# Spreading the gMLP layer-norm statistics and bias over four steps, with reordered top-k, modulation-row and query-pack work, in a one-core decoder block

## The chip, the cores and the metric

The kernel runs on one core of a Trainium2 chip. The metric is the time of one execution in microseconds (us), the median of three runs. A run of before was also recorded by the hardware profiler, and all views below are of that one execution.

## The reference, cut to what matters

One decoder layer over 512 positions of width 1024. The input is normalised and modulated by rows that come from a conditioning vector, then projected into ten pieces. The part that the change touches is mixer A, the gated MLP, and what runs beside it:

```python
h = rms_norm(x, norm1_g) * (1.0 + scale1) + shift1
z = h @ w_in                       # a_u, a_v, q, k, v, qi, ki, wi, g_a, g_b
...
v = layer_norm(gelu(a_v), ln_g, ln_b).reshape(bsz, n, 128, 8, 128)
mixed = einsum('gts,bnsgc->bntgc', w_s * tril, v) + b_s
y_a = gelu(a_u) * mixed
...
sel_score, sel_idx = lax.top_k(score, 256)      # per query, indexer scores
y_b = attention of q over the selected keys
...
merged = sigmoid(g_a) * (y_a @ w_proj_a) + sigmoid(g_b) * (y_b @ w_proj_b)
x = x + gate1 * (merged @ w_out)
```

A feed-forward part and a final norm follow. The layer norm's shift `ln_b` reaches the mixed output as `ln_b` times the row sums of the masked `w_s`, so the kernel computes these row sums (`wrow`) and adds them to `b_s` instead of adding `ln_b` to v.

## The kernel before

All large products are fp32 products made of three matmuls in a rounded fp32 form. Each weight chunk of 128x1024 numbers (512 KB) is loaded by SyncE into one of three `raw` buffers (`issue`, L149), rounded by ScalarE to `hi` (L167), and VectorE or GpSimd subtracts `lo = raw - hi` (L171). `hi` and `lo` have three buffers each. `mm3` (L107 to L109) then issues, for each pair of blocks, hi by h-hi, hi by h-lo, and lo by h-hi: the third matmul is the first that needs `lo`. `opt_b` runs over the chunks of a weight group; before each chunk it calls the step's side tasks and then `get`, which prepares the chunks up to two ahead. So the preparation of the chunk after next is emitted behind a step's side tasks, and stands behind them in the queues of ScalarE and VectorE.

The stages around the change, in the order of the program:

- the a_v stage, 14 steps whose side tasks are in the table `VT`. Among them: `wn_load`, `wn_mask` and `wn_sum` form the row sums of the masked spatial weights; `wn_out` (L1043) writes them to a DRAM scratch, turned; `wn_in` reads them back, one copy per partition, into `wr`; `load_ws` and `load_bs` load spatial weights and bias; `ln_v(tk, 0)` takes the statistics of the first half of v's columns.
- the a_u stage, steps 0 to 7 of `au_tasks`, two chunks of each of four groups `W_AU`, 24 matmuls a step. Step 0 finishes the layer norm's statistics (`ln_v(tk, 1)` for four blocks of rows), takes the power -1/2 on GpSimd (`rstd`), forms `nmr` and scales the bias rows on ScalarE (`bias_a`, eight instructions). Steps 1 and 2 normalise v in place on ScalarE (`ln_v2`), and step 2 adds the bias (`bias_b`). After step 3 TensorE mixes the first group (`mix_mm`, L1183), the others after steps 4 to 9; `mix_ev` takes them out on VectorE (L1189, L1192 and a split).
- steps 8 to 23: gate A (`W_GA`) and the projection of y_a (`W_PA`), two chunks each in turn, four times. Attention begins in step 22 (`at_step`), with `qk` products on TensorE and the softmax's first row operation on VectorE (L1319).

Three things run in the background of these steps. The top-k search is a list `bg` of 32 items, alternately `topk_max` (three MAX8, L862) and `topk_replace` (three MATCH_REPLACE8, L866), and three closing items; `run_bg(us)` pops items until their nominal costs exceed its budget. The modulation rows of gate 1 and of the second norm are dot products: SyncE loads 512 KB into `mraw` (L255) and VectorE multiplies and sums (L259). `room` decides how early such a load is issued: two may be outstanding before, in two buffers that alternate. The rows of q that are rotated are packed through DRAM (`Packed`): `gather`, `fetch`, `turn` on VectorE, `put` and `scatter`, where all DMAs are issued by GpSimd.

SyncE works through its DMA list in order, and a DMA whose buffer isn't free yet holds the ones behind it.

Of the kernel before, what the change touches and what calls it, by code (L numbers as in the profile page):

```python
# [58 lines left out]
def block_kernel(ctx: ExitStack, tc: tile.TileContext, x, x_t, w_in,  # L59
# [3 lines left out]
    T, V, A, P, SY = nc.tensor, nc.vector, nc.scalar, nc.gpsimd, nc.sync  # L63
# [63 lines left out]
    def issue(i):  # L127
        e = stream[i]
        if e["kind"] == "m" and e["early"]:
            k = mrot[0]  # L130
            mrot[0] += 1
            raw = s2pair(k % 8, F32).rearrange("p a n -> p (a n)")
        elif i in last_raw:
            raw = last_raw[i]()
        elif e["kind"] == "m" and e["mid"]:
            k = e["mid"]
            if k == "A2":
                k = ("A2", "G1")[mrot[1] % 2]
                mrot[1] += 1
            raw = mid.tile([128, 1024], F32, name="mraw", tag=k, bufs=1)  # L140
        else:
            raw = base.tile([128, 1024], F32, name="raw", tag="raw", bufs=RAWB)
        e["raw"] = raw
        if e["kind"] == "m":
            e["dma"](raw)
            return
        k0, nk, n = e["kts"][0], len(e["kts"]), e["n"]
        e["view"] = lambda t: t[:, :nk * n].rearrange("p (j n) -> p j n", j=nk)
        SY.dma_start(raw[:, :nk * n], e["src"](k0, nk, e["c0"] if isinstance(e["c0"], tuple) else ((e["c0"], n),)))  # L149
        if i in W1[2:7]:  # L150
            load_xt(W1.index(i) + 1)
# [22 lines left out]
    def ensure(upto):  # L174
        upto = min(upto, len(stream) - 1, st["limit"] - 1)
        while True:
            for i in range(st["prep"], min(st["prep"] + 16, len(stream), st["limit"])):
                if "raw" in stream[i]:
                    continue
                if room(i):  # L180
                    issue(i)
                elif stream[i]["kind"] == "w" or not stream[i]["mid"]:
                    break
            if st["prep"] > upto:
                break
            prep(st["prep"])
            st["prep"] += 1

    def room(i):
        e = stream[i]  # L190
        if i in last_raw:
            return True
        pend = [stream[k] for k in range(st["prep"], i) if k not in last_raw]
        if e["kind"] == "m" and e["early"]:
            return sum(p["kind"] == "m" for p in pend) < 8
        if e["kind"] == "m" and e["mid"]:
            n = sum(p["kind"] == "m" for p in pend)
            return n < (2 if e["mid"] == "A2" else 1) and len(pend) <= 1 + 2 * n
        return sum(p["kind"] == "w" or not (p["early"] or p["mid"]) for p in pend) < RAWB


# [216 lines left out]
    V.tensor_copy(cols[:, 0:67], pack[:, 0:67])  # L418
    posi = pack[:, 67:195].bitcast(I32)
    P.tensor_copy(half_sum[:, 16:32], pack[:, 195:211])  # L420
    lng, lnb, wrow = half_sum[:, 16:24], half_sum[:, 24:32], half_sum[:, 32:40]

    ones = mid.tile([128, 128], F32, name="ones", tag="A3", bufs=1)
    P.memset(ones, 1.0)
# [241 lines left out]
    class Packed:  # L666

        def __init__(self, tag, srcs):
            self.srcs, self.rows = srcs, 32 * len(srcs)
            self.d = [dram.tile([128, S], F32, name=f"pk{tag}{k}") for k in range(2)]  # L670

        def part(self, k, n):
# [10 lines left out]
        def fetch(self):  # L683
            t = at_line(base, "S2_4", (2, S), F32, "pk") if self.rows < 64 else mid.tile(
                [128, 2, S], F32, name="pk", tag="G0", bufs=1)
            self.a, self.b = t[:, 0], t[:, 1]
            for o, flip in ((self.a, 0), (self.b, 1)):
                for h in range(2):
                    k = self.rows * (h ^ flip)
                    src = self.d[0][k:k + self.rows]  # L690
                    if self.rows < 64:
                        src = src[None].to_broadcast([2, 32, S])
                    P.dma_start(o[64 * h:64 * h + 64], src)

        def turn(self):
            V.tensor_mul(self.b, self.b, tab["q"][:, 1])
# [1 line left out]
            V.tensor_add(self.a, self.a, self.b)  # L698

        def put(self):  # L700
            P.dma_start(self.d[1], self.a)

        def scatter(self):
            for j, t in enumerate(self.srcs):
                for h in range(2):
                    P.dma_start(t[16 * h:16 * h + 16], self.rows_of(1, 128, j, h))

    kf = mid.tile([128, 2, S], F32, name="kf", tag="A0", bufs=1)
    mid.tile([128, 16], F32, name="pad")
# [56 lines left out]
    def k_b(h):  # L766
        if not kk:
            k_tiles()
        split(kk[0][:, h], kk[1][:, h], kf[:, h])
        A.activation(k_pl[:, h], kf[:, h, :128], AF.Copy)  # L770
# [238 lines left out]
    def av_sum(g, key):  # L1009
        avr[g, key] = t = avr[g, {"T2": "T1", "T4": "T2"}[key]]  # L1010
        V.tensor_add(t, t, avr[g, {"T2": "B22", "T4": "B21"}[key]])

    def av_w(g, key):
        hi, lo = (base.tile([128, 4, 256], F32R, name=n, tag=n, bufs=3) for n in ("hi", "lo"))
        split(hi, lo, avr[g, key])
        avw[g, key] = (hi, lo)
# [22 lines left out]
    def wn_sum(h):  # L1039
        for k in range(4):  # L1040
            A.activation(wn[:, k], wn[:, k], AF.Copy, accum_out=wrow[:, 4 * h + k:4 * h + k + 1])

    def wn_out():  # L1043
        P.dma_start(wsd.rearrange("m t -> t m"), wrow)

    def wn_in():
        late["wr"] = mid.tile([128, 1024], F32, name="wr", tag="G1", bufs=1).rearrange("p (a n) -> p a n", a=8)
# [30 lines left out]
    def ln_v(tk, h):  # L1078
        V.bn_stats(bst[:, tk, h * 6:h * 6 + 6], vg[tk // 2][:, tk % 2, h * 512:(h + 1) * 512])
        if h:  # L1080
            V.bn_aggr(mva[:, tk], bst[:, tk, 0:12])
# [24 lines left out]
    def av_add(k, op, src):  # L1106
# [8 lines left out]
          5: [lambda: av_w(1, "B11"), pkk.put, lambda: wn_load(1)],  # L1115
          6: [lambda: av_w(1, "T1"), lambda: av_acc(1, "T3"), lambda: issue(W_AU[0][0])],
          7: [lambda: av_sum(1, "T2"), lambda: av_w(1, "T2"), pkk.scatter, wn_mask],
          8: [lambda: av_w(1, "B21"), lambda: wn_sum(1), wn_out],
          9: [lambda: av_w(1, "T3"), lambda: av_sum(1, "T4")],
          10: [lambda: av_w(1, "B22"), wn_in],  # L1120
          11: [lambda: av_w(1, "T4"), lambda: issue(W_AU[0][1]), lambda: ln_v(0, 0)],
          12: [lambda: ensure(W_AU[0][0]), lambda: ln_v(1, 0), lambda: ln_v(2, 0), load_ws, load_bs],
          13: [lambda: ensure(W_AU[0][1]), lambda: ln_v(3, 0), lambda: k_b(0), ws_mask]}

    def av_post(g, p):
        if p == 0:
# [80 lines left out]
    def au_tasks():  # L1207
        s = austep[0]
        austep[0] += 1
        if s == 0:  # L1210
            k_b(1)
        for fn in PT.get(s, []):
            fn()
        if s == 0:
            for tk in range(4):
                ln_v(tk, 1)
            rstd(rva, mva[:, :, 1], 4, 1.0)
            V.scalar_tensor_tensor(nmr, mva[:, :, 0], -1.0, rva, op0=OP.mult, op1=OP.mult)
            bias_a()
            run_bg(0.8)  # L1220
        elif s == 1:
            ln_v2(0)
            ln_v2(1)
        elif s == 2:
            ln_v2(2)
            ln_v2(3)
            bias_b()
        for m in AT.get(s - 1, []):
            mix_ev(m)
        if s > 0:  # L1230
            run_bg(1.6 if s < 8 else 2.0)
        if s in (20, 21):
            at_split(s - 20)

# [1056 lines left out]
```

## Time and profile before

| what | value |
|---|---|
| median of three runs | 790.62 us (789.58 to 792.36) |
| the profiled execution's own time | 790.31 us |
| its span, first to last instruction | 788.6 us |
| outside the span | 1.7 us |
| mean granted TensorE clock | 0.995 |
| busy: TensorE, VectorE, ScalarE, GpSimd | 771.6, 669.3, 448.3, 195.0 us |

TensorE (PE) has an instruction in flight for 98% of the span. VectorE is DVE in the views, ScalarE ACT, GpSimd POOL, SyncE SP; "SPq" and "POOLq" are their DMA issues. In a timeline row stand the start, the duration, the engine, the line, the instruction and the tiles, and in brackets how long the engine sat idle before it and what it waited for. TensorE's matmuls overlap: one of 512 columns is shown as 0.39 us long, while the next starts 0.23 us after it. The time lost to a late operand is therefore read from start to start.

### The profile page before, as it was taken

What the parts mean: (1) busy time and instruction counts of PE and PEld (TensorE: products, weight loads), DVE (VectorE), ACT (ScalarE), POOL (GpSimd) and SP (SyncE); (2) the same over time, 40 slices, a digit from 0 to 9 for tenths busy, and PEclk for the clock granted to TensorE, in tenths of its full rate; (3) what the DMA queues carried; (4) which work ended last, traced back from release to release, by engine and by line L of the source; (5) the groups of instructions that cost most, each with busy time, mean ns of one, the idle gap of its engine ahead of it and who ended that gap; (6) DMA issues with size and microseconds to landing.
All of it is one profiled execution on the core that took longest, in us unless ns stands there. A gap on an engine that the chain in (4) does not pass through costs nothing.

```text
span 788.6 us, 12719 instructions
## 1 busy us (share of the span) xinstructions
PE 771.6 (98%) x4723; PEld 692.3 (88%) x4723; DVE 669.3 (85%) x1108; ACT 448.3 (57%) x803; POOL 195.0 (25%) x274
## 2 busy tenths in 40 slices
PE   8999999989999999999999999999999999999995
PEld 6899899968888788998888899999999999888884
DVE  8879777898999758986697878989999888998886
ACT  6665567553231346666546577655566666666653
POOL 5882312132365521200020000313121212000002
PEclk9999999999999999999999999999999999999998
DMA  9966655525264848627682503879896977666662
GB/s 349 416 188 188 151 155 144 169 88 171 101 195 162 289 163 213 188 63 272 213 254 35 206 1 108 247 234 299 257 279 208 270 211 188 180 193 210 206 214 107
DMA packets 54561, 153.45 MB, mean 195 GB/s; under 512 B 15617, under 2 KB 16257, under 8 KB 54498
## 3 DMA queue, kind: packets, MB, share of 16 engines
q1 hardware_dynamic: 41552, 115.34, 43.4%
q0 software_dynamic: 12368, 36.33, 19.1%
q10 hardware_dynamic: 578, 0.95, 0.3%
q8 instruction: 37, 0.61, 0.3%
q14 instruction: 26, 0.21, 0.1%
HBM read 146.29 MB, written 28.72 MB: 222 GB/s over the span
## 4 chain that ended last, share of the span: by engine, by line
PE 81%; DVE 12%; DMA 2%; ACT 2%; issue 1%; POOL 1%; POOLq 0%; SPq 0%; ACTq 0%; DVEq 0%
PE R L108 8%; PE R L107 8%; PE R L109 8%; PE pb L109 5%; PE pb L108 5%; PE pb L107 5%; PE pfo L108 4%; PE pfo L109 4%; PE pfo L107 4%; DVE sco L866 3%; DVE m L862 2%; PE pgb L107 2%; PE pgb L108 2%; PE pgb L109 2%; DVE mraw L259 2%; PE po L107 2%
## 5 line engine op out<-in xcount | busy, mean ns | idle before, releaser
L167 ACT ACTIVATE hi<-raw 128x1024 fp32r<-128x1024 f32 (+4 forms) x98 | 98.6, 1010 | 87.0 <-PE pfo L109 23.6
L171 DVE TENSOR_TENSOR lo<-raw,hi 128x1024 fp32r<-128x1024 f32 (+2 forms) x71 | 84.9, 1198 | 25.6 <-ACT hi L167 25.5
L109 PE MATMUL pb<-h,lo 128*128 128x512 f32 (+1 forms) x192 | 73.9, 385 | 3.5 <-DVE lo L171 3.4
L107 PE MATMUL pb<-h,hi 128*128 128x512 f32 (+1 forms) x192 | 74.3, 387 | 0.0
L108 PE MATMUL pb<-h,hi 128*128 128x512 f32 (+1 forms) x192 | 73.7, 384 | 0.0
L171 POOL TENSOR_TENSOR lo<-raw,hi 128x1024 fp32r<-128x1024 f32 x19 | 48.0, 2533 | 63.1 <-ACT hi L167 63.1
L108 PE MATMUL pfo<-lo,za 128*128 128x512 f32 (+1 forms) x144 | 55.2, 383 | 0.0
L109 PE MATMUL pfo<-hi,za 128*128 128x512 f32 (+1 forms) x144 | 55.2, 383 | 0.0
L107 PE MATMUL pfo<-hi,za 128*128 128x512 f32 (+1 forms) x144 | 55.2, 383 | 0.0
L259 DVE CUSTOM_DVE_ANT_0 mraw<-mraw,csb,cols 128x1024 f32<-128x1024 f32 x27 | 43.2, 1601 | 6.2 <-DMA mraw<-in_w_shsc_dram 6.2
L109 PEld LDWEIGHTS pb<-h,lo 128*128 128x128 f32 x192 | 36.5, 190 | 10.9 <-DVE lo L171 4.0
L107 PE MATMUL R<-tb,sx 128*128 128x256 f32 x160 | 44.2, 276 | 0.0
L109 PE MATMUL R<-tb,sx 128*128 128x256 f32 x160 | 44.2, 276 | 0.0
L108 PE MATMUL R<-tb,sx 128*128 128x256 f32 x160 | 44.2, 276 | 0.0
L107 PE MATMUL R<-tb,hi 128*128 128x256 f32 x160 | 44.2, 276 | 0.0
L108 PE MATMUL R<-tb,hi 128*128 128x256 f32 x160 | 44.2, 276 | 0.0
L109 PE MATMUL R<-tb,lo 128*128 128x256 f32 x160 | 44.2, 276 | 0.0
L392 POOL COPY sm<-sm 128x1 f32<-128x1 f32 x36 | 23.8, 660 | 81.6 <-ACT sm L391 81.6
L108 PEld LDWEIGHTS pb<-h,hi 128*128 128x128 f32 x192 | 36.5, 190 | 6.2
L107 PEld LDWEIGHTS pb<-h,hi 128*128 128x128 f32 x192 | 36.4, 189 | 6.0
L372 POOL DMA_DIRECT2D wsum<-in_w_ffn_out_dram x24 | 19.6, 816 | 74.5 <-DMA wsum<-wsum 42.2
L107 PEld LDWEIGHTS pfo<-hi,za 128*128 128x128 f32 x144 | 27.1, 188 | 5.4
(426 smaller groups left out, 2672.9 us busy)
## 6 DMA issues: line engine op xcount, KB each, us to landing
raw<-in_w_ffn_in_dram SPq DMA_DIRECT2D x44, 512.0 KB, 6.4
raw<-in_w_in_dram SPq DMA_DIRECT2D x38, 512.0 KB, 4.3
wsum<-in_w_ffn_out_dram POOLq DMA_DIRECT2D x30, 512.0 KB, 7.7
mraw<-in_w_shsc_dram SPq DMA_DIRECT2D x27, 512.0 KB, 6.5
raw<-wsum SPq DMA_DIRECT2D x20, 512.0 KB, 3.6
s<-in_w_shsc_dram SPq DMA_DIRECT2D x14, 512.0 KB, 8.3
raw<-in_w_ffn_out_dram SPq DMA_DIRECT2D x13, 512.0 KB, 3.7
wsum<-wsum POOLq DMA_DIRECT2D x10, 512.0 KB, 6.7
```

Of the source, the lines that this page charges most:

```text
L107: T.matmul(o, wh, rh, start=start, stop=False, **kw)
L108: T.matmul(o, wh, rlo, start=False, stop=False, **kw)
L109: T.matmul(o, wlo, rh, start=False, stop=stop, **kw)
L167: A.activation(hi[:, :m], e["raw"][:, :m], AF.Copy)
L171: e["lo"].tensor_sub(lo[:, :m], e["raw"][:, :m], f(hi[:, :m]))
L259: V.tensor_tensor_reduce(out=raw[:, c], in0=raw[:, c], in1=(csb if s > 1 else pc)[:, c], scale=scale, scalar=sums.pop(0), op0=OP.mult, op1 ...
L372: P.dma_start(wsum_at(n, c), src, max_dma_last_dim=4096, accum_op=OP.add)
L392: P.tensor_copy(t, t)
L862: V.max(m8s[i], sco[i])
L866: V.match_replace(out=sco[i], in_to_replace=m8s[i], in_values=sco[i], imm_value=TAKEN)
```

## The change

Five edits, all between the a_v stage and step 23:

1. The second-half statistics are spread: blocks 0 and 1 in step 0, blocks 2 and 3 and the power in step 1, `nmr`, the first normalisation and the scaled bias rows in step 2, the second normalisation and the bias add in step 3. Before, statistics, power, `nmr` and scaled bias were all in step 0, and each normalisation a step earlier.
2. The row sums are accumulated in `gcol`, turned in 32x32 blocks on VectorE, and written out as four DMAs of rows instead of one DMA of single numbers. `wn_out`, `wn_in` and `load_bs` move a step later, and the mask of the spatial weights moves to step 0 of a_u.
3. The top-k budget is 0 in step 0 and 1.3 in steps 1 to 6 (one item a step, where there were two), and 2.0 from step 7 on.
4. `room` allows a modulation-row load only when no other is pending, so each is asked for one period later.
5. The fetch, put and scatter DMAs of the two query packs are issued by SyncE; those of the key pack and all gathers stay on GpSimd.

The core of the diff:

```diff
@@ room
         if e["kind"] == "m" and e["mid"]:
-            n = sum(p["kind"] == "m" for p in pend)
-            return n < (2 if e["mid"] == "A2" else 1) and len(pend) <= 1 + 2 * n
+            return all(p["kind"] == "w" for p in pend) and len(pend) <= 1
...
-    lng, lnb, wrow = half_sum[:, 16:24], half_sum[:, 24:32], half_sum[:, 32:40]
+    lng, lnb, wrow = half_sum[:, 16:24], half_sum[:, 24:32], gcol[:, 16:24]
@@ Packed
+            self.q = P if tag == "k" else SY
...
-                    P.dma_start(o[64 * h:64 * h + 64], src)
+                    self.q.dma_start(o[64 * h:64 * h + 64], src)
...
-            P.dma_start(self.d[1], self.a)
+            self.q.dma_start(self.d[1], self.a)
...
-                    P.dma_start(t[16 * h:16 * h + 16], self.rows_of(1, 128, j, h))
+                    self.q.dma_start(t[16 * h:16 * h + 16], self.rows_of(1, 128, j, h))
@@
     def wn_out():
-        P.dma_start(wsd.rearrange("m t -> t m"), wrow)
+        V.transpose(gturn, gcol)
+        rows = wsd.rearrange("m (b j) -> m b j", j=32)
+        for b in range(4):
+            P.dma_start(rows[:, b], gturn[32 * b + 16:32 * b + 24])
@@ VT
-          8: [lambda: av_w(1, "B21"), lambda: wn_sum(1), wn_out],
-          9: [lambda: av_w(1, "T3"), lambda: av_sum(1, "T4")],
-          10: [lambda: av_w(1, "B22"), wn_in],
-          11: [lambda: av_w(1, "T4"), lambda: issue(W_AU[0][1]), lambda: ln_v(0, 0)],
-          12: [lambda: ensure(W_AU[0][0]), lambda: ln_v(1, 0), lambda: ln_v(2, 0), load_ws, load_bs],
-          13: [lambda: ensure(W_AU[0][1]), lambda: ln_v(3, 0), lambda: k_b(0), ws_mask]}
+          8: [lambda: av_w(1, "B21"), lambda: wn_sum(1)],
+          9: [lambda: av_w(1, "T3"), lambda: av_sum(1, "T4"), wn_out],
+          10: [lambda: av_w(1, "B22")],
+          11: [lambda: av_w(1, "T4"), lambda: issue(W_AU[0][1]), lambda: ln_v(0, 0), wn_in],
+          12: [lambda: ensure(W_AU[0][0]), lambda: ln_v(1, 0), lambda: ln_v(2, 0), load_ws],
+          13: [lambda: ensure(W_AU[0][1]), lambda: ln_v(3, 0), lambda: k_b(0), load_bs]}
@@ au_tasks
         if s == 0:
+            ws_mask()
             k_b(1)
...
-            for tk in range(4):
-                ln_v(tk, 1)
+            ln_v(0, 1)
+            ln_v(1, 1)
+        elif s == 1:
+            ln_v(2, 1)
+            ln_v(3, 1)
             rstd(rva, mva[:, :, 1], 4, 1.0)
+        elif s == 2:
             V.scalar_tensor_tensor(nmr, mva[:, :, 0], -1.0, rva, op0=OP.mult, op1=OP.mult)
-            bias_a()
-            run_bg(0.8)
-        elif s == 1:
             ln_v2(0)
             ln_v2(1)
-        elif s == 2:
+            bias_a()
+        elif s == 3:
             ln_v2(2)
             ln_v2(3)
             bias_b()
...
-            run_bg(1.6 if s < 8 else 2.0)
+            run_bg(1.3 if s < 7 else 2.0)
```

How the instructions stand on VectorE at the start of the a_u stage, before. `kin` holds the statistics, `mva` mean and variance, `m` and `sco` belong to the top-k search, and the `lo` here is that of the third chunk, which step 2 multiplies with:

```order
L1079 BN_STATS kin<-vg_1147 128x6
L1081 BN_AGGR mva<-kin 128x2
L1079 BN_STATS kin<-vg_1147 128x6
L1081 BN_AGGR mva<-kin 128x2
L1218 SCALAR_TENSOR_TENSOR sm<-mva,sm 128x4
L862 MAX m_1813<-sco_633 128x8
L862 MAX m_1815<-sco_632 128x8
L862 MAX m_1817<-sco_631 128x8
L171 TENSOR_TENSOR lo<-raw,hi 128x1024
L866 MATCH_REPLACE sco_633<-m_1813,sco_633 128x512
```

The same place now, from the first block's statistics on:

```order
L1082 BN_STATS kin<-vg_1146 128x6
L1084 BN_AGGR mva<-kin 128x2
L1082 BN_STATS kin<-vg_1146 128x6
L1084 BN_AGGR mva<-kin 128x2
L171 TENSOR_TENSOR lo<-raw,hi 128x1024
L1082 BN_STATS kin<-vg_1147 128x6
L1084 BN_AGGR mva<-kin 128x2
L1082 BN_STATS kin<-vg_1147 128x6
L1084 BN_AGGR mva<-kin 128x2
L862 MAX m_1838<-sco_633 128x8
L862 MAX m_1840<-sco_632 128x8
L862 MAX m_1842<-sco_631 128x8
```

The third chunk's `lo` has moved ahead of two of the four statistics, the `nmr` instruction (which waits for GpSimd's power) and the MAX8 triple. On ScalarE, at the same place, now: the normalisation (`vg`) of step 2 stands behind the first gelu output `u`, and the eight scaled bias rows `wr` behind the first normalisation:

```order
L167 ACTIVATE hi<-raw 128x1024 x2
L1245 ACTIVATE u<-pb 128x512 x2
L1174 ACTIVATE vg_1146<-vg_1146,sm 128x1024 x2
L1055 ACTIVATE wr<-wr,half_sum 128x128 x8
L167 ACTIVATE hi<-raw 128x1024
L1174 ACTIVATE vg_1147<-vg_1147,sm 128x1024 x2
L167 ACTIVATE hi<-raw 128x1024
L1245 ACTIVATE u<-pb 128x512 x2
```

Before, the eight `wr` came ahead of the third chunk's `hi`, and both normalisations ahead of the second `u`. On GpSimd the `lo` subtractions of steps 3 to 21 had the query packs' DMAs between them before:

```order
L171 TENSOR_TENSOR lo<-raw,hi 128x1024 x2
L706 DMA qf_602<-pkq_613 16x2x512 x2
L706 DMA qf_603<-pkq_613 16x2x512 x2
L693 DMA pk<-pkq_1150 64x512 x4
L171 TENSOR_TENSOR lo<-raw,hi 128x1024 x4
```

Now one row stands there, `lo` nineteen times over, and the DMAs are in SyncE's list between the weight loads. TensorE's order is the same in both kernels.

## Prediction

> **What bounds the kernel now.** I read the page's head, then TensorE's waits, then the chain of waits, then the timelines around the places those named.
>
> ```profile
> span 788.6 us, 12719 instructions
> PE pb L109 <- DVE lo L171: 3.4, 1, 3.4
> PE pb L109 <- POOL lo L171: 1.4, 1, 1.4
> ```
>
> After its start TensorE sits idle twice, both times for a `lo`, until the end of the span. So the change can gain only what the two cost, and whatever TensorE loses too briefly to be listed. Since matmuls overlap, I measure from start to start. TensorE's timeline around the first wait:
>
> ```profile
> 160.96 0.39 PE L107 MATMUL pb<-h,hi 128*128 128x512 f32 x1
> 161.19 0.39 PE L108 MATMUL pb<-h,hi 128*128 128x512 f32 x1
> 165.00 0.50 PE L109 MATMUL pb<-h,lo 128*128 128x512 f32 x1 [3.42 <-DVE lo L171]
> ...
> 166.08 0.63 PE L107 MATMUL pb<-h,hi 128*128 128x512 f32 x1
> 166.51 0.63 PE L108 MATMUL pb<-h,hi 128*128 128x512 f32 x1
> ...
> 169.44 0.39 PE L109 MATMUL pb<-h,lo 128*128 128x512 f32 x1
> ```
>
> A matmul normally starts 0.23 us after the last (160.96 to 161.19). Step 2 of a_u starts at 160.96, and its third matmul is late. From 161.19 to 169.44 there are 13 starts: 8.25 us where 13 x 0.227 = 2.95 would do. **5.3 lost**, of which 1.4 because seven matmuls behind the wait follow each other at 0.43, a halved clock. The other two places:
>
> ```profile
> 233.61 0.39 PE L108 MATMUL pb<-h,hi 128*128 128x512 f32 x1
> 234.08 0.50 PE L109 MATMUL pb<-h,lo 128*128 128x512 f32 x1
> ...
> 261.19 0.40 PE L108 MATMUL pb<-y,hi 128*128 128x512 f32 x1
> 262.98 0.50 PE L109 MATMUL pb<-y,lo 128*128 128x512 f32 x1 [1.40 <-POOL lo L171]
> ```
>
> The first loses 0.47 - 0.23 = **0.24**, the second 1.79 - 0.23 = **1.56**. All three make 7.1 us.
>
> The chain of waits tells why the two `lo` are late:
>
> ```profile
> 136.25 10.28 DMA wrow<-half_sum
> ...
> 162.34 1.47 DVE m L862 x3
> 163.82 1.12 DVE lo L171
> ...
> 204.00 1.59 DVE sco L866 x4
> ...
> 210.95 1.59 DVE sco L866 x4
> ...
> 249.81 2.67 DVE mraw L259
> 252.52 0.33 SPq L255
> 252.94 6.37 DMA raw<-in_w_proj_a_dram
> ```
>
> Step 0's statistics, GpSimd's power and a MAX8 triple stand ahead of the third chunk's `lo`; earlier, the write of the row sums as single numbers takes 10.28 and holds up GpSimd's list. The later wait comes through SyncE: a row load (L255) is issued only when VectorE, running late, has consumed that buffer (249.81 to 252.48), and the weights for step 18 are queued behind it.
>
> **The change, part by part.** A step has 24 matmuls, 24 x 0.227 = 5.45 us. VectorE's and ScalarE's timelines in step 0 and 1:
>
> ```profile
> 157.49 0.69 DVE L1079 BATCH_NORM_STATS2 kin<-vg 128x6 f32<-128x512 f32 x1
> 162.26 0.16 DVE L1218 SCALAR_TENSOR_TENSOR sm<-mva,sm 128x4 f32<-128x4 f32 x1 [1.44 <-POOL sm L436]
> 156.34 2.44 ACT L1052 ACTIVATE wr<-wr,half_sum 128x128 f32<-128x128 f32 x8
> 158.68 1.05 ACT L167 ACTIVATE hi<-raw 128x1024 fp32r<-128x1024 f32 x1
> 162.52 2.37 ACT L1171 ACTIVATE vg<-vg,sm 128x1024 f32<-128x1024 f32 x2 [2.80 <-DVE sm L1218]
> ```
>
> *First wait.* Four statistics take from 157.49 to 162.26 - 1.44 = 160.82, 0.83 each. Now come two of them (1.7) and then the third `lo` (1.1): its `hi` waited for no data at 158.68, and the eight `wr` (2.44) no longer stand ahead of it. So `lo` ends at 157.5 + 1.7 + 1.1 = 160.3; the matmul wants it at 161.42. It fits by 1.1. The 5.3 go, the halved clock among them. Late next would be the fourth `lo`, behind two statistics and a MAX8 triple: 160.3 + 1.7 + 1.4 + 1.1 = 164.5; step 3 wants it at 160.96 + 5.45 = 166.4. It fits too.
>
> *The next wait in line* is the first mixing product, which needs all of v normalised. ScalarE, now: first half of v once `nmr` is there (164.6), 2.4 to 167.0; eight `wr` to 169.4; a `hi` to 170.4; second half to 172.8. Without the stall the mixing starts at 160.96 + 48 x 0.227 = 171.9, and the third of its four matmuls is the first to read the second half. That is a wait of up to 0.8, or none if the freed GpSimd list lets VectorE run ahead. I take 0.3 and keep 0 to 0.8. The mask of the spatial weights in step 0 costs nothing: GpSimd has nothing else until the power.
>
> *Row sums.* One turn of 32 columns on VectorE and four small DMAs. The turn lies in the a_v stage behind TensorE's products; uncovered it would cost less than the 1.1 of a `lo`, with 1024 columns. For the issues and the query packs, GpSimd's timeline:
>
> ```profile
> 229.52 2.08 POOL L693 DMA_DIRECT2D pk<-pkq  x4
> 231.59 4.77 POOL L171 TENSOR_TENSOR lo<-raw,hi 128x1024 fp32r<-128x1024 f32 x2
> ```
>
> Four issues take GpSimd 2.1; behind those of the row sums stand only the mask of the scores and the read-back, which then no longer wait for 10.28. On the path: nothing.
>
> *Query packs on SyncE.* Two `lo` at 231.59 stood behind such issues, which is the 0.24: gained. SyncE's list gets 18 issues of 0.33, 6 us over 13 steps; each weight load is asked for about two steps (11 us) before its use against 6.37 to land, so that much is hidden. Put waits for a turn made two steps earlier, scatter for a write one or two steps old, and the weight loads stand behind both. I take 0 and keep up to 1.6, the size of the present wait through SyncE.
>
> *Row loads a period later.* With one load outstanding and two buffers, a load goes where the product is a whole step old, so SyncE no longer waits for the one being made: 1.56 gained. VectorE may wait for rows to land instead, as it does now for 4.9 us in all:
>
> ```profile
> L259 DVE CUSTOM_DVE_ANT_0 mraw<-mraw,csb,cols 128x1024 f32<-128x1024 f32 x15 | 27.6, 1843 | 4.9 <-DMA mraw<-in_w_shsc_dram 4.9
> L1281 DVE TENSOR_TENSOR part<-pb,sg 128x512 f32<-128x512 f32 x6 | 3.8, 679 | 0.0
> 216.97 0.48 PE L107 MATMUL pb<-y,hi 128*128 128x512 f32 x1
> 292.65 0.39 PE L107 MATMUL qk<-k_hi,qh 128*128 128x512 f32 x1
> ```
>
> *Top-k later.* Seven items of about 1.5 (1.47 and 1.59 above), 10 us of VectorE, move from steps 0 to 6 to steps 16 to 19. Is VectorE still done in time? Step 10 starts at 216.97 - 5.3 = 211.7. A step with mixing, a MAX and MATCH pair and a product takes VectorE 6.95 (204.00 to 210.95); if it starts 3 us late, step 10 is done at 221.7. Left then: eight pairs of 3.0, eleven products of at most 1.8, gate products 3.8, and as much again for a turn, closing items and splits: 52 us, to 273.5. The third `qk` product (292.65, now 285.5) needs the bank that the first softmax row reads, 1.3 of work: wanted by 284.2. VectorE has 10.7 us to spare, so the later search costs nothing.
>
> **A rule against the change.** One of the 15 products:
>
> ```profile
> 231.90 5.55 DVE L259 CUSTOM_DVE_ANT_0 mraw<-mraw,csb,cols 128x1024 f32<-128x1024 f32 x1
> ```
>
> It lay beside GpSimd's two `lo` (231.59 to 236.36) and ended after them, at three times the mean of 1.84; a MAX8 or MATCH triple doesn't stretch like that. Now fewer top-k items fill the time of GpSimd's `lo` in steps 1 to 6. The Trainium skill, GPSIMD Engine Reference, section Key points, says that GpSimd shares its SBUF interfaces with VectorE and contends with instructions that have two SBUF inputs; the trace agrees with 5.55 against 1.84. By that rule the kernel would go the way of the third rival.
>
> The halved clock after 3.42 idle, and none after 1.40, is the other thing that a rule bears on. The Trainium skill, TensorE: Matmul & The Clock Gate, section Part 1, says that the clock falls after an idle window of about 3.4 us that runs free of the program. By that rule some executions of before lack the 1.4, and against those the gain is 5.4 rather than 6.8.
>
> **The sum.** -5.3 - 0.24 - 1.56 + 0.3 = -6.8. The span goes from 788.6 to 781.8, the profiled execution from 790.31 to 783.5. The median of before is 790.62, 0.31 above it, and so I predict **783.8 us**; the unknowns at their ends give 783.5 to 785.9.
>
> **Rivals.** 0.3% (2.4 us) is about what can be told from no change, so faster is below 788.2.
>
> 1. *Only the first wait goes* (0.22): weights stand behind put and scatter as they stood behind the row load, or the halved clock wasn't in the median. For it: SyncE still works in order, and waits for VectorE's turn. Against: what it waits for is a step or two old. 790.6 - 5.3 + 0.3 = 785.6; with one more wait of 1.6, 787.2.
>
> 2. *The wait moves to the mixing, or the statistics weren't what held `lo`* (0.10). If the power, the bias read-back or the weights' mask come 4 us later than counted, ScalarE's list stands still and the mixing waits for 3.4, with the halved clock again. For it: 2.44 of `wr` now stands between the halves of v. Against: all three are asked for no later than before. 790.6 - 7.1 + 3.4 + 1.4 = 788.3, so 787 to 790.
>
> 3. *Slower: GpSimd's `lo` against VectorE's products* (0.04). Each of the eleven products from step 11 on waits out a whole `lo` (2.4, half of 4.77) beyond its 1.84: 26 us more against 10.7 to spare. It decides from 1.0 a product. TensorE then waits 15.7 at the third `qk`: 790.6 - 7.1 + 15.7 + 1.4 = 800.6; at half of it 792. Against: the 1.84 already holds today's share of this, and the pile-up of two `lo` behind DMA issues is gone.
>
> **How the numbers follow.** My forecast has 0.64 (782.3 to 785.9). The range of 782.0 to 787.5 holds it, rival 1 and a little of rival 2, about 0.87; its low end is the sum without the 0.3 and with 1.5 of spread between runs. Faster: 0.64 + 0.22 + 0.04 of rival 2 = 0.90; same: the rest of rival 2, 0.06; slower: 0.04.
>
> **What would show it.** Right: no 3.4 in TensorE's waits and no spacing of 0.43 after 160; the third `lo` ends before 160.5; the row-sum write takes 2 to 4; the mixing starts near 172; GpSimd's nineteen `lo` have no DMA rows among them; no SyncE load waits on L259. Wrong: a wait on L1183 (rival 2); waits for `lo` at steps 16 to 20 with SyncE standing on a put or scatter (rival 1); products of L259 near 4 us and `qk` waiting for L1319 (rival 3).

## The result, and the profile after

| | before | after |
|---|---|---|
| median, us | 790.57 (789.58 to 792.36, 4 runs) | 781.59 (781.29 to 781.80, 4 runs) |
| profiled execution, us | 790.31 | 781.80 |
| its span, us | 788.6 | 780.1 |
| outside the span, us | 1.7 | 1.7 |

The ratio is 0.9884, 95% interval 0.9865 to 0.9902. The forecast was 783.8 with a range of 782.0 to 787.5: the direction was right, and 9.0 us went where 6.8 were foretold. The time lies 0.4 below the range.

From the page of after, the head, TensorE's waits and the start of the chain's shares:

```profile
span 780.1 us, 12714 instructions
PE warm L544 <- POOL ones L423: 3.3, 1, 3.3
PE 98%; DVE 0%; DMA 0%; issue 0%; POOL 0%; ACT 0%; POOLq 0%
```

Behind its start (the `warm` wait is at 3 us and is in before too) no wait of TensorE is listed any more, and 98% of the chain of waits runs along TensorE. VectorE's timeline in steps 0 and 1:

```profile
157.47 1.21 DVE L171 TENSOR_TENSOR lo<-raw,hi 128x1024 fp32r<-128x1024 f32 x1
...
160.24 1.43 DVE L862 MAX8 m<-sco 128x8 f32<-128x512 f32 x3
161.59 1.21 DVE L171 TENSOR_TENSOR lo<-raw,hi 128x1024 fp32r<-128x1024 f32 x1
162.71 0.15 DVE L1226 SCALAR_TENSOR_TENSOR sm<-mva,sm 128x4 f32<-128x4 f32 x1
```

The third `lo` starts at 157.47, where in before it started at 163.73, and the `nmr` instruction (L1226) no longer stands idle for GpSimd. At the mixing, ScalarE and then TensorE:

```profile
168.47 2.36 ACT L1174 ACTIVATE vg<-vg,sm 128x1024 f32<-128x1024 f32 x2
```

```profile
171.88 0.39 PE L109 MATMUL pb<-h,lo 128*128 128x512 f32 x1
172.10 1.05 PE L1186 MATMUL mix<-wmT,vg 128*128 128x128 f32 x8
```

The second half of v is ready at 170.83, and the mixing starts at 172.10 without a wait.

*Where the time came from.* TensorE's order is the same in both kernels, so two fixed matmuls can be timed in each: a product of a_v (L108) and one of y (L109). Before, then after:

```profile
149.73 0.28 PE L108 MATMUL pav<-lo,h 128*128 128x256 f32 x1
...
297.23 0.39 PE L109 MATMUL pb<-y,lo 128*128 128x512 f32 x1
...
779.81 0.28 PE L109 MATMUL pfo<-wx,zl 128*128 128x256 f32 x1
```

```profile
150.07 0.28 PE L108 MATMUL pav<-lo,h 128*128 128x256 f32 x1
...
290.05 0.39 PE L109 MATMUL pb<-y,lo 128*128 128x512 f32 x1
...
772.43 0.28 PE L109 MATMUL pfo<-wx,zl 128*128 128x256 f32 x1
```

Between them lie 147.51 us before and 139.98 after: **7.53 of the gain are here**, call it the stage. By the same rows after reaches the stage 0.35 later, and gains 0.20 between the stage and the last matmul. The later start isn't the change's doing: the traces of all thirteen other kernels reach that matmul between 149.99 and 150.24, whichever edits they have, and only the one of before at 149.73. From the last matmul to the end of the span are 788.6 - 779.81 = 8.8 before and 780.1 - 772.43 = 7.7 after, 1.1 less. 7.53 - 0.35 + 0.20 + 1.1 = 8.5, which is the whole difference of the two profiled executions. The medians lie 9.0 apart; the other 0.5 is between them and the profiled executions.

### The profile page after: what moved, and what is told of

Read it like the earlier page. It is cut to its first block, busy times and chain, and to the rows that moved or that the text cites. A ratio compares the mean times of both kernels' runs of the same rounds, so it can differ in the third digit from the quotient of the medians.

```text
span 780.1 us, 12714 instructions
## 1 busy us (share of the span) xinstructions
PE 769.3 (99%) x4723; PEld 692.7 (89%) x4723; DVE 662.8 (85%) x1109; ACT 448.9 (58%) x803; POOL 184.4 (24%) x259
## 4 chain that ended last, share of the span: by engine, by line
PE 98%; DVE 0%; DMA 0%; issue 0%; POOL 0%; ACT 0%; POOLq 0%
PE pb L107 9%; PE pb L108 9%; PE pb L109 9%; PE R L107 8%; PE R L109 8%; PE R L108 8%; PE pfo L109 4%; PE pfo L107 4%; PE pfo L108 4%; PE pgb L107 2%; PE pgb L108 2%; PE pgb L109 2%; PE po L107 2%; PE po L108 2%; PE po L109 2%; PE pav L108 2%
## 5 line engine op out<-in xcount | busy, mean ns | idle before, releaser
L171 DVE TENSOR_TENSOR lo<-raw,hi 128x1024 fp32r<-128x1024 f32 (+2 forms) x71 | 82.9, 1169 | 29.8 <-ACT hi L167 29.5
L108 PE MATMUL pb<-h,hi 128*128 128x512 f32 (+1 forms) x192 | 73.0, 380 | 0.0
L109 PE MATMUL pb<-h,lo 128*128 128x512 f32 (+1 forms) x192 | 73.0, 380 | 0.0
L171 POOL TENSOR_TENSOR lo<-raw,hi 128x1024 fp32r<-128x1024 f32 x19 | 45.5, 2398 | 68.1 <-ACT hi L167 65.1
L108 PE MATMUL pfo<-lo,za 128*128 128x512 f32 (+1 forms) x144 | 55.2, 383 | 0.0
L109 PE MATMUL pfo<-hi,za 128*128 128x512 f32 (+1 forms) x144 | 55.2, 383 | 0.0
L258 DVE CUSTOM_DVE_ANT_0 mraw<-mraw,csb,cols 128x1024 f32<-128x1024 f32 x27 | 41.3, 1531 | 4.3 <-DMA mraw<-in_w_shsc_dram 4.3
L109 PE MATMUL R<-tb,sx 128*128 128x256 f32 x160 | 44.2, 276 | 0.0
L109 PE MATMUL R<-tb,lo 128*128 128x256 f32 x160 | 44.2, 276 | 0.0
L108 PE MATMUL R<-tb,hi 128*128 128x256 f32 x160 | 44.2, 276 | 0.0
L108 PE MATMUL R<-tb,sx 128*128 128x256 f32 x160 | 44.2, 276 | 0.0
L109 PEld LDWEIGHTS pb<-h,lo 128*128 128x128 f32 x192 | 36.0, 188 | 6.3
L108 PEld LDWEIGHTS pb<-h,hi 128*128 128x128 f32 x192 | 36.1, 188 | 5.9
L108 PEld LDWEIGHTS pfo<-lo,za 128*128 128x128 f32 x144 | 27.1, 188 | 5.3
```

Source lines behind the costliest of these rows:

```text
L108: T.matmul(o, wh, rlo, start=False, stop=False, **kw)
L109: T.matmul(o, wlo, rh, start=False, stop=stop, **kw)
L171: e["lo"].tensor_sub(lo[:, :m], e["raw"][:, :m], f(hi[:, :m]))
L258: V.tensor_tensor_reduce(out=raw[:, c], in0=raw[:, c], in1=(csb if s > 1 else pc)[:, c], scale=scale, scalar=sums.pop(0), op0=OP.mult, op1 ...
```

## Experiments

The first theory, once the trace of after was known: VectorE runs behind TensorE through steps 0 to 20, and each wait is that lateness coming through at the place that can bear it least. Then the edits don't add: taking one cause away lets the next wait appear, and two edits that each remove the same lateness pay once. The rival is the forecast's own way: one edit, one wait, and the terms add.

All kernels are timed against before, in five rounds. "Stage" is the time between the two matmuls above, less that of after (7.53 for before); it is read from one profile each, and e3 and e5 agree there with after to 0.00.

| kernel | edits in it | median, us | ratio to before, 95% interval | stage, us more than after |
|---|---|---|---|---|
| before | none | 789.57 to 791.74 | 1 | 7.53 |
| e1 | 1 | 788.29 | 0.9978 [0.9969, 0.9987] | 5.97 |
| e12 | 2 | 785.45 | 0.9948 [0.9935, 0.9960] | 4.02 |
| e11 | 3 | 785.58 | 0.9954 [0.9940, 0.9968] | 2.81 |
| e6 | 4 | 795.25 | 1.0038 [1.0023, 1.0052] | 12.20 |
| e9 | 1, 3 | 784.39 | 0.9909 [0.9886, 0.9933] | 1.98 |
| e10 | 1, 2, 3 | 782.44 | 0.9910 [0.9896, 0.9924] | 0.39 |
| e13 | 2, 3, 4, 5 | 782.23 | 0.9882 [0.9866, 0.9899] | 0.45 |
| e2 | 1, 2, 4, 5 | 784.19 | 0.9919 [0.9904, 0.9933] | 2.15 |
| e3 | 1, 2, 3, 5 | 781.62 | 0.9889 [0.9873, 0.9904] | 0.00 |
| e4 | 1, 2, 3, 4 | 782.49 | 0.9901 [0.9885, 0.9916] | 0.81 |
| e5 | all, 2 with the old DMA | 782.01 | 0.9875 [0.9851, 0.9900] | 0.00 |
| e7 | all, 1 in part | 781.69 | 0.9873 [0.9851, 0.9895] | 0.14 |
| after | all | 781.59 | 0.9884 [0.9865, 0.9902] | 0 |

An interval is about 0.7 to 1.9 us to each side, so differences under that are read from the stage and its waits, not from the medians.

### One edit alone, on the kernel before

**e1, the statistics and bias spread (edit 1).** The first lines of its `au_tasks`:

```diff
-            for tk in range(4):
-                ln_v(tk, 1)
-            rstd(rva, mva[:, :, 1], 4, 1.0)
-            V.scalar_tensor_tensor(nmr, mva[:, :, 0], -1.0, rva, op0=OP.mult, op1=OP.mult)
-            bias_a()
+            ln_v(0, 1)
+            ln_v(1, 1)
             run_bg(0.8)
         elif s == 1:
+            ln_v(2, 1)
+            ln_v(3, 1)
+            rstd(rva, mva[:, :, 1], 4, 1.0)
...
```

> Before with edit 1 alone (statistics, power, normalisation and bias spread over four steps), the top-k item of step 0 kept. If the parts of the sum are independent: the third chunk's lo ends 160.3 + 1.4 for the MAX8 triple = 161.7 against 161.4 wanted, so the first wait shrinks to 0.3 and the time falls by 5.0 to 785.6, the waits at 234 and 261 staying as they are. If VectorE's debt decides (it was saturated from step 2 to 17 and gains only 1.4 us itself): TensorE now runs 5 us earlier into the same late row products, the later wait grows from 1.6 to 4 or more, and 787 to 789 is left.

TensorE's waits and ScalarE's timeline at the mixing, in e1:

```profile
PE pb L109 <- POOL lo L171: 2.5, 3, 1.3
PE mix L1183 <- ACT vg L1171: 1.8, 2, 1.2
```

```profile
167.22 2.38 ACT L1171 ACTIVATE vg<-vg,sm 128x1024 f32<-128x1024 f32 x2 [5.19 <-DVE sm L1223]
...
172.80 1.23 ACT L1171 ACTIVATE vg<-vg,sm 128x1024 f32<-128x1024 f32 x1
```

The 3.4 is gone, and only 7.53 - 5.97 = 1.6 of it stays gained. TensorE, no longer held, comes to the mixing earlier, and there ScalarE has stood 5.19 for VectorE's `nmr`; three waits for GpSimd's `lo` follow, where before had two places. The wait moved, as the second rival had it, though the rest of the change prevents that. The time is that of the second branch of the expectation, but not the place: the wait near 261 was to grow to 4, and it is 1.26.

**e12, the row sums (edit 2).** It has `wn_out` by turn and rows, the moved `wn_in` and `load_bs`, and the mask of the spatial weights in step 0.

```diff
-        P.dma_start(wsd.rearrange("m t -> t m"), wrow)
+        V.transpose(gturn, gcol)
...
         if s == 0:
+            ws_mask()
             k_b(1)
```

> Kernel before with edit 2 alone (row sums turned on VectorE, the mask of the spatial weights out of the a_v stage; statistics, top-k, row loads and packs as before). The forecast had this edit at nothing on the path: 790.6. If VectorE's start on the statistics is what it brings forward, by the 1.7 seen in the changed kernel, the first wait falls from 3.4 to about 1.7 and the halved clock goes, 3.1 in all; with VectorE as late as before from there on, up to 1.5 of it is given back in later waits: 787.5 to 789.

TensorE's waits, then VectorE's timeline, in e12:

```profile
PE pb L109 <- POOL lo L171: 1.5, 1, 1.5
PE pb L109 <- DVE lo L171: 1.5, 1, 1.5
```

```profile
155.82 0.69 DVE L1082 BATCH_NORM_STATS2 kin<-vg 128x6 f32<-128x512 f32 x1
...
160.60 0.16 DVE L1222 SCALAR_TENSOR_TENSOR sm<-mva,sm 128x4 f32<-128x4 f32 x1 [1.45 <-POOL sm L436]
...
162.07 1.21 DVE L171 TENSOR_TENSOR lo<-raw,hi 128x1024 fp32r<-128x1024 f32 x1
```

The statistics start at 155.82 instead of 157.49, everything behind them is 1.7 earlier, the wait is 1.5 instead of 3.4, and no matmul behind it is spaced 0.43. The stage gains 3.5. The two later places stay as they were (0.24 and 1.70 from start to start), so nothing was given back, where I had expected up to 1.5. The forecast had put this edit's place on the path at nothing.

Why VectorE starts earlier stands on GpSimd in the a_v stage. GpSimd and VectorE in before, then GpSimd in e12:

```profile
147.10 0.57 POOL L1048 DMA_DIRECT2D wr<-wrow  x1 [9.91 <-DMA wrow<-half_sum]
147.67 0.30 POOL L855 TENSOR_SCALAR_AFFINE_SELECT sco<-sco 128x128 f32<-128x128 f32 x1
148.01 0.43 DVE L862 MAX8 m<-sco 128x8 f32<-128x256 f32 x1 [1.92 <-POOL sco L855]
```

```profile
143.15 0.30 POOL L855 TENSOR_SCALAR_AFFINE_SELECT sco<-sco 128x128 f32<-128x128 f32 x1
```

In before the mask of the scores (L855) stands behind the read-back of the row sums (L1048), which waits for their write (in e6 and e9 for a product of a_v), and VectorE's MAX8 stands 1.92 for that mask. With `wn_in` a step later the mask goes first, and the MAX8 doesn't wait. The traces of all fourteen kernels bear this out: the five without edit 2 have a wait of 1.3 to 2.4 here and begin the second-half statistics at 157.2 to 158.9, the nine with it have none and begin at 155.7 to 156.0. The mask of the spatial weights, which moved too, isn't the cause: no wait of VectorE is put down to it. The move of `wn_in` alone wasn't run.

**e11, the thinner top-k (edit 3).**

```diff
-            run_bg(0.8)
...
-            run_bg(1.6 if s < 8 else 2.0)
+            run_bg(1.3 if s < 7 else 2.0)
```

> Kernel before with edit 3 alone (no top-k item in step 0, one instead of two in steps 1 to 6). The forecast had this edit at nothing: 790.6. If VectorE's lateness is what links the waits, the third lo of a_u comes a MAX8 triple of 1.47 earlier (first wait 3.4 to about 2, perhaps without the 1.4 of halved clock) and the late waits of 0.24 and 1.56 shrink or go: 786 to 788.

TensorE's waits, then VectorE's timeline, in e11:

```profile
PE pb L109 <- DVE lo L171: 1.9, 1, 1.9
PE pb L109 <- POOL lo L171: 0.3, 1, 0.3
```

```profile
162.51 0.16 DVE L1218 SCALAR_TENSOR_TENSOR sm<-mva,sm 128x4 f32<-128x4 f32 x1 [1.44 <-POOL sm L436]
162.62 1.22 DVE L171 TENSOR_TENSOR lo<-raw,hi 128x1024 fp32r<-128x1024 f32 x1
```

Nothing stands between `nmr` and the `lo` any more. The stage gains 4.7, more than any other edit alone: the halved clock goes with the shorter wait, and the two late waits shrink from 1.80 to 0.44, read from start to start, though neither the row loads nor the packs were touched. The time lies 0.4 under the expected 786 to 788.

**e6, the row loads a period later (edit 4).**

```diff
-            n = sum(p["kind"] == "m" for p in pend)
-            return n < (2 if e["mid"] == "A2" else 1) and len(pend) <= 1 + 2 * n
+            return all(p["kind"] == "w" for p in pend) and len(pend) <= 1
```

> Before with edit 4 alone, modulation rows asked for a period later. If the parts are independent: the 1.6 us wait at step 18 goes, the first wait stays, 788.8. If VectorE's debt decides: SyncE no longer waits for it, but VectorE waits for rows to land and is later still, and the wait shows up elsewhere: 790 to 791.

TensorE's waits in e6, then GpSimd's timeline, then VectorE's:

```profile
PE pb L109 <- DVE lo L171: 4.0, 2, 3.7
PE pb L107 <- DVE part L1280: 3.4, 2, 2.3
```

```profile
228.58 2.04 POOL L705 DMA_DIRECT2D qf<-pkq  x4
230.61 2.07 POOL L692 DMA_DIRECT2D pk<-pkq  x4
232.69 7.11 POOL L171 TENSOR_TENSOR lo<-raw,hi 128x1024 fp32r<-128x1024 f32 x3
```

```profile
232.99 7.89 DVE L258 CUSTOM_DVE_ANT_0 mraw<-mraw,csb,cols 128x1024 f32<-128x1024 f32 x1
...
240.81 1.28 DVE L1280 TENSOR_TENSOR part<-pb,sg 128x512 f32<-128x512 f32 x2
```

Slower, by 4.7 in the stage, and by more than either expectation had (795.25 against 790 to 791 at most). Some 0.8 of that is lost by the end of the first wait: the read-back of the row sums goes out at 147.91 in this trace, and the MAX8 behind the mask of the scores (see e12) waits 2.42 instead of 1.92. That is hardly the edit's doing, since e9, without it, has nearly the same (147.76 and 2.21). The rest comes from the place shown. Eight DMA issues (4.1) have piled up three `lo` on GpSimd. The row product that now meets them takes 7.89 where a free one takes 1.27, and the gate products (`part`) stand behind it; they hold TensorE's bank, 1.2 here and 2.3 at the next pair; between the two VectorE has no idle time. This is the third rival's mechanism, on one product rather than on eleven. The Trainium skill, SBUF — State Buffer, section SBUF: two separate sides, says that GpSimd and a VectorE instruction with two SBUF inputs exclude each other for a whole instruction. This trace agrees: the product ends at 240.88, 1.08 after the third `lo` (239.80).

### One edit taken out of the changed kernel

**e13, the statistics back in step 0 (edit 1 out).** `au_tasks` takes back the four statistics, the power, `nmr` and the scaled bias in step 0.

```diff
-            ln_v(0, 1)
-            ln_v(1, 1)
-        elif s == 1:
-            ln_v(2, 1)
-            ln_v(3, 1)
+            for tk in range(4):
+                ln_v(tk, 1)
             rstd(rva, mva[:, :, 1], 4, 1.0)
-        elif s == 2:
...
```

> Changed kernel with edit 1 taken back: the four statistics, the power, its result and the scaled bias all in step 0, normalisations in steps 1 and 2; no top-k item in step 0 (edits 2 to 5 stay). If the edits add as in the forecast, edit 1 is worth 5.3 and the time is 781.6 + 5.3 = 786.9. If VectorE's lateness is what counts, edits 2 and 3 have already brought the third lo forward by 1.7 and 1.5: statistics end near 159.2, the power is there at 160.6, lo ends near 161.9 against 161.4 wanted, so 0.5 and a restart of 0.1 are lost: 782.2. A wait at the mixing can't come, since bias and normalisation are where they were before: no L1183 among the waits in either case.

TensorE's only wait behind its start, and VectorE's timeline, in e13:

```profile
PE pb L109 <- DVE lo L171: 0.2, 1, 0.2
```

```profile
160.66 0.16 DVE L1222 SCALAR_TENSOR_TENSOR sm<-mva,sm 128x4 f32<-128x4 f32 x1 [1.45 <-POOL sm L435]
160.76 1.23 DVE L171 TENSOR_TENSOR lo<-raw,hi 128x1024 fp32r<-128x1024 f32 x1
```

The edit after which the whole change is named is worth 0.45 in the stage once the others are there; the forecast had it at 5.3. Edits 2 and 3 had brought the `lo` forward by 1.7 and 1.5 already.

**e2, the old top-k budget (edit 3 out).** The diff is that of e11, turned round.

> After with the old top-k budget (one item in step 0, two a step in steps 1 to 7). If the thinner top-k is only cover: the third lo is 0.3 late and the rest as after, 781.6 to 782. If VectorE's debt decides: the last mixing rows (which were 1.8 us early before) are late for the projection of step 11 by 2 to 4 us, and the time is 783.5 to 786.

TensorE's waits in e2:

```profile
PE mix L1186 <- ACT vg L1174: 0.6, 1, 0.6
PE pb L109 <- POOL lo L171: 0.5, 1, 0.5
```

2.15 come back in the stage, at the mixing and at GpSimd's `lo` near 225. The time is that of the second branch of the expectation, the places are not: it had named the last mixing rows. Of the edits taken out of the changed kernel it is the dearest; edit 2 was taken out in its form alone (e5).

**e3, the old row loads (edit 4 out).** The diff is that of e6, turned round.

> After with the old rule of when a modulation row is asked for (two outstanding). If the parts are independent: SyncE waits for the row product again and TensorE loses the 1.6 us at step 18, 783.2. If VectorE's debt decides, which after no longer has: SyncE finds the buffer free early enough, no wait, 781.6.

781.62, no wait of TensorE in the stage, 0.00. Edit 4 is worth nothing here.

**e4, the query packs back on GpSimd (edit 5 out).**

```diff
-            self.q = P if tag == "k" else SY
+            self.q = P
```

> After with the query packs' fetch, put and scatter on GpSimd again. If GpSimd's DMA issues between its lo subtractions cost TensorE what they did before: 0.3 us at step 13, 781.9. If GpSimd has enough slack once VectorE isn't late: 781.6, no wait at step 13.

TensorE's wait and the row products (count, then shortest, median and longest in ns) in e4, then those of after:

```profile
PE pb L107 <- DVE part L1287: 0.5, 1, 0.5
```

```profile
L258 DVE CUSTOM_DVE_ANT_0 mraw<-mraw,csb,cols x5: 1270/1835/5561, 225.0 to 252.1; 128x1024 f32<-128x1024 f32 x5
```

```profile
L258 DVE CUSTOM_DVE_ANT_0 mraw<-mraw,csb,cols x15: 1267/1274/3265, 200.0 to 274.2; 128x1024 f32<-128x1024 f32 x15
```

The pile-up is back, and with it a product of 5.56; the worst of the same products in after takes 3.27. Edit 5 is worth 0.8 in the stage, with a wait for VectorE. That the 5.56 leads to this wait isn't shown: the gate products that TensorE waits for at 256.12 stand right behind another product, of 3.26, and e10 has one of 5.57 without such a wait. The forecast saw only the two late `lo`, 0.24, and neither expectation had a loss through VectorE.

**e5, the row sums as single numbers, at the new places.**

```diff
-        V.transpose(gturn, gcol)
-        rows = wsd.rearrange("m (b j) -> m b j", j=32)
-        for b in range(4):
-            P.dma_start(rows[:, b], gturn[32 * b + 16:32 * b + 24])
+        P.dma_start(wsd.rearrange("m t -> t m"), wrow)
```

> After with the row sums written as single numbers by one DMA again, at their new places. If the 10 us write matters only through GpSimd's list and nothing is queued behind it any more but the read-back: 781.6, no wait of TensorE. If the read-back into the scaled bias comes too late for ScalarE: the first mixing product waits 1 to 2 us, 782.6 to 783.6.

No wait in the stage, 0.00. So what e12 gained doesn't hang on the form of the DMA: with the new places the mask of the scores (141.81) goes ahead of the read-back (148.16), and the old write holds up nobody.

**e7, the statistics together, the power left in step 1.** All four `ln_v(tk, 1)` and a top-k item stand in step 0 again, `rstd` in step 1, the rest as in after.

```diff
-            ln_v(0, 1)
-            ln_v(1, 1)
+            for tk in range(4):
+                ln_v(tk, 1)
+            run_bg(0.8)
         elif s == 1:
-            ln_v(2, 1)
-            ln_v(3, 1)
```

> After with all four statistics and one top-k item in step 0 again, the power still in step 1, so that VectorE doesn't wait for GpSimd ahead of the third lo. The lo ends 160.3 + 1.7 + 1.4 = 163.4 against 161.4 wanted: an idle time of 1.6 to 2.0, too short for the halved clock of before. If the halved clock needs some 3.4 us of idle time: 783.6, spacing 0.23 behind the wait. If any such wait halves the clock: 785.

VectorE's timeline in e7:

```profile
159.22 1.43 DVE L862 MAX8 m<-sco 128x8 f32<-128x512 f32 x3
160.57 1.21 DVE L171 TENSOR_TENSOR lo<-raw,hi 128x1024 fp32r<-128x1024 f32 x1
```

All four statistics and a MAX8 triple stand ahead of the third `lo`, and it costs 0.14. My expectation of a renewed wait was wrong. With the other edits in, spreading the statistics isn't what matters in edit 1; not standing 1.44 for GpSimd's power ahead of the `lo` is enough.

### Combinations

**e9, edits 1 and 3.**

> Before with edits 1 and 3 (statistics spread, thinner top-k in steps 0 to 6), without the edits of row sums, row loads and query packs. If the parts are independent: the first wait goes, the later ones stay, 785.3. If VectorE's debt decides, paying it back also removes the later wait through SyncE: 782.5 to 783, about what after has with the packs on GpSimd.

TensorE's waits in e9:

```profile
PE mix L1183 <- ACT vg L1171: 0.6, 1, 0.6
PE pb L109 <- POOL lo L171: 0.4, 1, 0.4
```

The stage gains 7.53 - 1.98 = 5.6. Alone the two gain 1.6 and 4.7. The median of 784.39 lies between the two branches of the expectation (785.3 and 782.5 to 783) and supports neither as it stood.

**e10, edits 1, 2 and 3**, with row loads and packs as before.

> Changed kernel with edits 4 and 5 taken back (row loads and query packs as before; edits 1, 2 and 3 stay). If the edits simply add, with the forecast's terms, both late waits are back: 0.24 + 1.56, so about 783.4 from the 781.6 of the changed kernel. If what counts is how far VectorE runs behind TensorE, and edits 2 and 3 have brought it back in time, the row loads cost nothing here either and only the 0.9 of the packs comes back: 782.5, with at most one wait of TensorE, under 1 us, for GpSimd's lo or VectorE's gate product.

0.39 in the stage, one start 0.25 late at 256.34. Against e9, edit 2 is worth 1.6 beside edits 1 and 3. Edits 4 and 5 together are worth 0.4. Edit 4 without 5 (e4, 0.81) is worse than neither (0.39).

## Why the prediction was right, and where it failed

**Right: what the first wait was, and that the later ones would fit.** The third `lo` was forecast to end before 160.5; it ends at 158.7, earlier than the 160.3 worked out, since VectorE also starts on the statistics 1.7 earlier. The mixing was to start near 172; it starts at 172.10. No 3.4, no spacing of 0.43. The page's group of GpSimd's `lo` in after, then GpSimd's timeline at the row sums:

```profile
L171 POOL TENSOR_TENSOR lo<-raw,hi 128x1024 fp32r<-128x1024 f32 x19 | 45.5, 2398 | 68.1 <-ACT hi L167 65.1
```

```profile
141.09 2.06 POOL L1047 DMA_DIRECT2D wrow<-gturn  x4 [12.14 <-DVE gturn L1044]
...
144.75 0.56 POOL L1051 DMA_DIRECT2D wr<-wrow  x1 [1.29 <-PE pav L108]
```

The nineteen `lo` average 2.40, and the read-back at 144.75 waits for TensorE, not for the row-sum write. None of the three rivals happened in the changed kernel, though e1 shows the second's move to the mixing and e6 the third's contention.

**The step that failed is the sum: -5.3 - 0.24 - 1.56 + 0.3, with "On the path: nothing" for the row sums and no term behind the last matmul.** Three things are wrong in it.

*Its size.* In the stage the change gains 7.53, not 6.8. The 0.3 for the mixing wasn't paid: `nmr` comes at 162.71 and not at 164.6, mostly because VectorE is 1.7 ahead through edit 2, which the forecast had at nothing. (e9, without edit 2, does wait 0.6 at the mixing.) The matmul behind a wait starts late too, 0.34 instead of 0.23 (163.90 to 164.24 in e11, behind a wait without halved clock). The 5.3 holds this, the 0.24 and the 1.56 don't, which makes 0.2 more: 7.1 + 0.2 = 7.3. The last 0.2 is made of differences under 0.1 that I can't place. With 7.5 instead of 6.8 the forecast would have been 783.1.

*What it left out.* The forecast said that the change "can gain only what the two cost, and whatever TensorE loses too briefly to be listed". But the span goes on behind the last matmul, for 8.8 before and 7.7 after, and the sum had no term for that 1.1. This tail goes with edit 2 in the fourteen profiles, one of each kernel: it is 8.4 to 8.8 long in the five kernels without it (before, e1, e6, e9, e11) and 7.3 to 8.1 in the nine with it. The difference stands behind SyncE's last issue of an output write: from there to the end of the span are 4.7 to 4.8 without edit 2 and 3.6 to 4.3 with it. The kernels run the same program there, so why it is shorter stays open; the form of the DMA isn't it, since e5 is among the nine. Between the stage and the last matmul the shift from after varies by -0.6 to +1.2 without following an edit. The low end of the range took 7.1 where 7.5 was to be had in the stage, nothing behind it, and 1.5 for spread, and so ended 0.4 too high.

*Its form.* The terms were put down to one edit each, and the total came nearly right although most of them were wrong:

| edit | forecast | alone (stage) | taken out of after (stage) |
|---|---|---|---|
| 1, statistics | -5.3 | -1.6 | +0.45 |
| 2, row sums and mask | 0 | -3.5 | 0.00 (form of the DMA alone, e5); +1.6 beside 1 and 3 alone (e9 against e10) |
| 3, top-k later | 0 | -4.7 | +2.15 |
| 4, row loads | -1.56 | +4.7 | 0.00 |
| 5, packs | -0.24 | not tried | +0.8 |

Of before's 3.4, three causes stood in one queue ahead of the `lo`: VectorE's late start, the stand for GpSimd's power, and the MAX8 triple. Without the late start alone the wait is 1.5 (e12), without the triple alone 1.9 (e11); without the late start and one of the other two almost nothing is left (0.45 in e13, 0.14 in e7). The stand for the power wasn't taken away alone. Alone, edits 1 to 3 gain 9.8, together 7.1 (e10). Three of the forecast's lines don't hold. It saw that the mask of the scores would no longer wait behind the row-sum write, and put that at nothing; it missed that VectorE's MAX8 stood for this mask, and that this cost 1.7 of VectorE's start. "The later search costs nothing" is true of its late end, and missed what the earlier, fuller search cost at the start. And the 1.56 was the lateness of VectorE, not the rule by which a row load is asked for: with edit 3 alone the late waits shrink to 0.44, and with edit 4 alone they grow. Nor did the sign for it come, that no SyncE load waits for the product: in after, from 150 to 290 us, the row loads still wait for it 10 times, 22.0 in all (12 times and 58.6 before).

The theory of VectorE's lateness carries this: edit 1 without 2 and 3 gives much of its gain back from the mixing on (e1), and edit 3 is the dearest of those taken out (e2). The additive rival falls with e13 (786.9 by it, 782.23 measured), e1 and e6. What stays open: why edit 4 hurts so much alone was traced to one product and the pair behind it, but whether a shift of a microsecond would have missed GpSimd's pile-up wasn't tried. Whether some executions of before run without the halved clock can't be said from its one trace. No run is told from after as faster; TensorE has no wait left in the stage to take away.

## What to carry to other kernels

When several waits trace back to one engine that runs late, cost the lateness, not the waits: an instruction that leaves that engine's queue early pays at the next place that would have waited, and the edits don't add. Ask of each wait everything that stands ahead of the late instruction, back to where its engine last had nothing to do; here that was a mask of the scores on GpSimd, in the stage before, held up by a write that it didn't need. And a transfer that comes later isn't free merely because its consumer has time: the consumer may meet other work, as in e6, where it met three GpSimd subtractions.

## What the runs showed of the hardware

*A wait shorter than 3.4 halves the clock too.* TensorE's timeline in e6, behind the wait of 2.25:

```profile
263.30 0.39 PE L109 MATMUL pb<-h,lo 128*128 128x512 f32 x1
265.94 0.47 PE L107 MATMUL pb<-y,hi 128*128 128x512 f32 x1 [2.25 <-DVE part L1280]
...
266.81 0.63 PE L107 MATMUL pb<-y,hi 128*128 128x512 f32 x1
267.24 0.63 PE L108 MATMUL pb<-y,hi 128*128 128x512 f32 x1
```

Matmuls follow at 0.43 from 266.81. Behind the 1.91 of e11 they don't. The Trainium skill, TensorE: Matmul & The Clock Gate, section Part 1, gives an idle window of about 3.4 us; by that no wait of 2.25 should do it, and the measurement decides. The clock falls only some 0.9 after the restart: until 266.81 the starts are 0.31, 0.23 and 0.33 apart. The granted clock of the trace says the same: it is 0.50 from 266.6 to 270.0, and in before from 165.9 to 169.4, 3.4 both times. Whether the length of the wait decides or the moment at which it falls isn't shown; 1.91 and 2.25 are one case each.

*The price of a row product* beside GpSimd's `lo` (2.40 each) goes by the number of `lo` that it waits out: 1.27 at the shortest (e4), 3.27 at the most in after, where it waits out the second of two, 5.55 beside two in before, 7.89 beside three in e6. That is a step of 2.0 to 2.3, about one `lo`. In these cases the product ends 1.1 behind the last `lo` of the pile (before, after, e6); that a pile costs VectorE more in all than the same `lo` one by one isn't shown.
